# The first FFN pair by plain products over token halves, with P1 and P2 of the next two pairs between the halves

## The chip, the cores and the metric

The kernel runs on one core of a Trainium2 chip. The metric is the device time of one execution in microseconds (us), the median over several. All times below are us unless marked ns. In the profile the engines are PE (TensorE matmul), PEld (its weight loads), DVE (VectorE), ACT (ScalarE), POOL (GpSimd) and SP (SyncE), on whose queue this kernel issues its DMAs.

## The reference, cut to what matters

One layer of an encoder trunk over 1024 tokens of width 1024. Two attention branches are merged and projected, then layer norm 1 makes `x1`, then a SwiGLU FFN with 2816 hidden channels, then layer norm 2:

```
x   = layer_norm(ALPHA * x + mix, ln1_g, ln1_b)
g, u = split(x @ w_ffn_in)                 # 1024 -> 2 * 2816
ffn = (silu(g) * u) @ w_ffn_out
out = layer_norm(ALPHA * x + ffn, ln2_g, ln2_b)
```

Everything is float32. The change lies at the seam between layer norm 1 and the product `x @ w_ffn_in`.

## The kernel before

Float32 products are made of float32r operands. `split` (L102 to L104) cuts a tile into a high part, rounded by ACT (L103), and a low part, the difference, by DVE (L104). A product is then three matmuls: high by high, high by low, low by high. One such matmul has 128x128 weights and 512 columns.

The hidden channels come in 22 blocks of 128. Block f needs a left weight tile (gate, `wLf`) and a right one (up, `wRf`), each 1024 x 128. The two belong together as a pair: the 1024 input features in two halves, the tokens in two halves and the two tiles make a 2x2 block product, done with seven products P1 to P7 in place of eight (a Winograd scheme). Each product is 4 feature slices by 3 matmuls, so 12 matmuls; a pair is 84. `pair_steps` (L168) gives the seven steps in the order P1, P2, P6, P5, P7, P3, P4. P1 and P2 use only the first token half: `x1A` tiles of features 0 to 511 (A10) and 512 to 1023 (A11). P6 and P3 use sums of blocks (`x1S63`), P5 and P7 others (`x1S57`), and P4 uses `x1A22`, the second feature half of the second token half. Accumulators in PSUM are `sx` (tag "mm", two banks), `sy` and `sz` (tag "sc", two banks). The pair's results are combined in SBUF tiles `gt` and `h` (tag "yt", three slots), and `h` is stored to DRAM.

The weights need sums too. `prep_left` loads `wLf` and splits it (`wl`). `prep_right` loads `wRf`, makes `ta` and `tb` from left and right tile with four DVE subtractions (L140 to L144), and splits both (`wa`, `wb`). `prep_last` splits half of `wRf` (`wc`). The raw tiles share three slots of tag "gt", so a load waits until an earlier raw tile has had its last reader.

The seam goes so. W_out (L823 ff.) runs over eight token tiles of 128 in two passes; in the second, each token tile gets its layer norm and is stored (`x1_dr`, on SP). After token tile 3 and again after tile 7, `x1_operands` (L741) transposes four tiles to feature-major (`x1ps`, three PSUM banks of tag "tr") and makes the operands. For the first token half that is the split `x1A` tiles and a raw copy; for the second half, in four rounds `kt`, the sums `x1s13` and `x1s24` (L764 to L771), the split of `x1A22`, and the splits of both sums.

`run_pairs` (L360) then lays out the FFN's order: P1 and P2 of pair 0, P1 and P2 of pair 1, the other five steps of pair 0, the other five of pair 1, then all seven steps of pair 2 and so on. Between steps it places the weight work of later pairs. The program is written in this order, and a scheduler moves instructions within each engine's queue where their operands allow. Each engine runs its queue in order.

The lines that the change touches are `run_pairs`, `x1_operands`, `right_f`, and the calls at the seam.

Of the kernel before, what the change touches and what calls it, by code (L numbers as in the profile page):

```python
# [12 lines left out]
F32R = mybir.dt.float32r  # L13
AF = mybir.ActivationFunctionType
ALU = mybir.AluOpType
# [3 lines left out]
P = 128  # L19
# [7 lines left out]
NF = D_FF // P  # L27
# [4 lines left out]
LO, HI = slice(0, HW), slice(HW, 2 * HW)  # L32
# [14 lines left out]
def hybrid_trunk_kernel(ctx: ExitStack, tc, x, xt, w_in, b_gate, rel_bias, w_proj,  # L47
# [6 lines left out]
    nc = tc.nc  # L54
# [7 lines left out]
    def slot(tag, name, dtype=F32):  # L62
        return pool.tile([P, 1024], dtype, tag=tag, name=name, bufs=SLOTS[tag])
# [10 lines left out]
    def bank(tag, name):  # L74
        return ps.tile([P, HW], F32, tag=tag, name=name, bufs=BANKS[tag])
# [6 lines left out]
    dma = nc.sync.dma_start  # L82
# [19 lines left out]
    def split(dst_h, dst_l, src):  # L102
        nc.scalar.copy(dst_h, src)  # L103
        nc.vector.tensor_tensor(dst_l, src, dst_h.bitcast(F32), ALU.subtract)  # L104
# [22 lines left out]
    def split_w(raw, nm, tag):  # L127
        h = slot(tag, f"{nm}h", F32R)
        l = slot(tag, f"{nm}l", F32R)
        split(h, l, raw)  # L130
        return h, l
# [15 lines left out]
    def prep_last(W, nm, tag):  # L147

        c = slot(tag, f"wc{nm}", F32R)
        split(c[:, LO], c[:, HI], W["R"][:, HI])  # L150
        W["c"] = c
# [205 lines left out]

        return pair_steps(f"p{i}", Wa[i], ops_x, c, done)

    def run_pairs(steps, left, right, also=lambda i: None):  # L360

        n = len(steps)
        for i in range(n):
            if i < 2:
                for j in ((0, 1) if i == 0 else ()):
                    steps[j][0]()
                    steps[j][1]()
                rest = steps[i][2:]
            else:
                rest = steps[i]  # L370
            for j, p in enumerate(rest):
                p()
                if j == 0 and i + 1 < n:
                    right(i + 1)
                if j == 1 and i + 2 < n:
                    left(i + 2)
            also(i)
# [360 lines left out]
            done(slice(0, D))  # L738

    ops_1 = {p: [] for p in range(1, 8)}  # L740
    x1raw = []  # L741

    def x1_operands(hf, acc_t):

        for kt in range(4):
            tps = []
            for k in (kt, kt + 4):
                tp = bank("tr", f"x1ps{hf}_{k}")
                for j in range(4):
                    tr(tp[:, j * P:(j + 1) * P], acc_t[4 * hf + j][:, k * P:(k + 1) * P], ident)  # L750
                tps.append(tp)
            if hf == 0:
                raw = slot("op", f"x1raw{kt}")
                for i in range(2):
                    o = slot("xt", f"x1A1{i}_{kt}", F32R)
                    split(o[:, LO], o[:, HI], tps[i])
                    nc.scalar.copy(raw[:, (LO, HI)[i]], tps[i])
                    ops_1[1 + i].append((o[:, LO], o[:, HI]))
                x1raw.append(raw)
            else:  # L760
                raw = x1raw[kt]
                s13 = slot("kp", f"x1s13_{kt}")
                s24 = slot("kp", f"x1s24_{kt}")
                nc.scalar.copy(s13[:, LO], tps[1])  # L764
                nc.vector.tensor_tensor(s13[:, HI], raw[:, LO], tps[0], ALU.subtract)
                nc.vector.tensor_tensor(s13[:, LO], tps[0], s13[:, LO], ALU.add)
                o = slot("bw", f"x1A22_{kt}", F32R)
                split(o[:, LO], o[:, HI], tps[1])
                ops_1[4].append((o[:, LO], o[:, HI]))
                nc.vector.tensor_tensor(s24[:, LO], s13[:, LO], raw[:, LO], ALU.subtract)  # L770
                nc.vector.tensor_tensor(s24[:, HI], raw[:, HI], s24[:, LO], ALU.subtract)  # L771
                for src, pa, pb, tags in ((s24, 6, 3, ("xt",)), (s13, 5, 7, QKV)):
                    h = cycle(tags, f"x1S{pa}{pb}h_{kt}", F32R)
                    l = cycle(tags, f"x1S{pa}{pb}l_{kt}", F32R)
                    split(h, l, src)
                    ops_1[pa].append((h[:, LO], l[:, LO]))
                    ops_1[pb].append((h[:, HI], l[:, HI]))
# [8 lines left out]
    def left_f(f):  # L786
        prep_left(Wf[f], f"f{f}", w_ffn_in[f])

    def right_f(f):
        prep_right(Wf[f], f"f{f}", w_ffn_in[NF + f], ("bw", "pt")[f % 2])  # L790
        if f:
            prep_last(Wf[f], f"f{f}", "op")

    def up_steps(f):

        tl = {}

        def c(name):

            if name == "12":  # L800
                if "h" not in tl:
                    tl["h"] = slot("yt", f"h{f}")
                return tl["h"][:, LO]
            if "t" not in tl:
                tl["t"] = slot("yt", f"gt{f}")
            return tl["t"][:, LO if name == "11" else HI]

        def done(name, acc):
            if name == "11":
                nc.scalar.activation(c("11"), c("11"), AF.Silu)  # L810
            elif name == "12":
                nc.vector.tensor_tensor(c("12"), c("12"), c("11"), ALU.mult)
            elif name == "21":
                h = tl["h"]
                nc.scalar.activation(h[:, HI], acc, AF.Silu)
                nc.vector.tensor_tensor(h[:, HI], h[:, HI], c("22"), ALU.mult)
                dma(h_dr[f], h)

        return pair_steps(f"f{f}", Wf[f], ops_1, c, done)

    for half_k in range(2):
        wo = [load_w(w_out[(4 * half_k + j) * P:(4 * half_k + j + 1) * P, :], f"o{half_k}_{j}",
                     of("gt"), of("xt"), nc.vector) for j in range(4)]  # L823
        if half_k == 1:
            left_f(0)
            right_f(0)
            left_f(1)
        for tt in range(8):
            ts_ = slice(tt * P, (tt + 1) * P)
            for hf, cs in enumerate((LO, HI)):  # L830
                acc = bank("mm" if hf == 0 else "sc", f"ops{half_k}_{tt}_{hf}")
                mm3(acc, [(mh[4 * half_k + j][:, ts_], ml[4 * half_k + j][:, ts_],
                           wo[j][0][:, cs], wo[j][1][:, cs]) for j in range(4)])
                nc.vector.scalar_tensor_tensor(
                    acc_t[tt][:, cs], acc_t[tt][:, cs], ALPHA if half_k == 0 else 1.0, acc,
                    ALU.mult, ALU.add)
            if half_k == 1:
                layer_norm(acc_t[tt], g1, b1, f"1_{tt}", tt % 4 >= 2)
                dma(x1_dr[tt], acc_t[tt])
                if tt % 4 == 3:  # L840
                    x1_operands(tt // 4, acc_t)

    prep_last(Wf[0], "f0", "op")
    run_pairs([up_steps(f) for f in range(NF)], left_f, right_f)


    groups = [(0, 2), (2, 6), (6, 10), (10, 14), (14, 18), (18, 22)]
# [62 lines left out]
```

## Time and profile before

| | us |
|---|---|
| runs | 1521.20, 1521.59, 1526.46; median 1521.59 |
| the profiled execution | 1521.58, its span 1519.8 |
| PE busy | 1468.8 (97%) |
| DVE busy | 912.2 (60%) |
| ACT busy | 644.9 (42%) |
| POOL busy | 277.3 (18%) |

The profiled execution stands 0.01 us below the median of the runs, and 1.8 us of it lie outside the span. PE is the engine to look at: it is busy for 97% of the span. A busy share says little of a seam of 25 us in 1520, though. For that one follows the chain of work that ended last, the waits and the engines' rows in that window.

### The profile page before, as it was taken

What the parts mean: (1) busy time and instruction counts of PE and PEld (TensorE: products, weight loads), DVE (VectorE), ACT (ScalarE), POOL (GpSimd) and SP (SyncE); (2) the same over time, 40 slices, a digit from 0 to 9 for tenths busy, and PEclk for the clock granted to TensorE, in tenths of its full rate; (3) what the DMA queues carried; (4) which work ended last, traced back from release to release, by engine and by line L of the source; (5) the groups of instructions that cost most, each with busy time, mean ns of one, the idle gap of its engine ahead of it and who ended that gap; (6) DMA issues with size and microseconds to landing.
All of it is one profiled execution on the core that took longest, in us unless ns stands there. A gap on an engine that the chain in (4) does not pass through costs nothing.

```text
span 1519.8 us, 18815 instructions
## 1 busy us (share of the span) xinstructions
PE 1468.8 (97%) x6884; PEld 1211.4 (80%) x6884; DVE 912.2 (60%) x1496; ACT 644.9 (42%) x1108; POOL 277.3 (18%) x315
## 2 busy tenths in 40 slices
PE   8899999999999999899999899999999999999997
PEld 6688888877778888777788688888888888888886
DVE  7755553577776665665748975555555537354437
ACT  6444443677666655764403533333333334021201
POOL 0000000433355544842305000000000000000016
PEclk9999999999999999999999899999999999999999
DMA  6555546765553445757602132222222248132202
GB/s 208 152 181 167 166 133 196 211 191 167 154 155 112 125 132 159 223 195 282 231 25 82 71 119 83 83 81 84 83 83 83 83 158 291 47 125 97 70 3 109
DMA packets 60189, 205.24 MB, mean 135 GB/s; under 512 B 7728, under 2 KB 7728, under 8 KB 60096
## 3 DMA queue, kind: packets, MB, share of 16 engines
q1 hardware_dynamic: 60096, 204.03, 41.1%
q8 instruction: 54, 0.88, 0.2%
q14 instruction: 39, 0.32, 0.1%
HBM read 142.63 MB, written 61.37 MB: 134 GB/s over the span
## 4 chain that ended last, share of the span: by engine, by line
PE 48%; DVE 2%; POOL 0%; DMA 0%; issue 0%; ACT 0%; POOLq 0%; DVEq 0%; ACTq 0%
PE sxf L165 15%; PE szf L165 8%; PE fps L113 5%; PE fps L111 5%; PE fps L110 5%; PE syf L165 4%; PE ops L113 2%; PE ops L111 2%; PE ops L110 2%; DVE bn L725 0%; DVE x1S57l L104 0%; DVE acc L732 0%; DVE x1S63l L104 0%; PE x1ps L750 0%; POOL mv L728 0%; DMA ln1b<-in_ln_b_dram 0%
## 5 line engine op out<-in xcount | busy, mean ns | idle before, releaser
L728 POOL TENSOR_TENSOR mv<-mv,neghalf 128x1 f32<-128x1 f32 x16 | 23.6, 1473 | 698.0 <-DVE mv L727 698.0
L110 PE MATMUL fps<-wh_fo,wh_h 128*128 128x512 f32 x352 | 137.0, 389 | 0.0
L113 PE MATMUL fps<-wh_fo,wl_h 128*128 128x512 f32 x352 | 137.0, 389 | 0.0
L111 PE MATMUL fps<-wl_fo,wh_h 128*128 128x512 f32 x352 | 136.9, 389 | 0.0
L872 DVE TENSOR_TENSOR x<-fps,x 128x512 f32<-128x512 f32 x80 | 54.9, 688 | 95.8 <-PE fps L113 95.8
L520 POOL TENSOR_TENSOR w_b<-w_b,kp_b 128x511 f32<-128x511 f32 (+3 forms) x96 | 97.0, 1016 | 75.1 <-DVE kp_b L518 63.7
L404 PE MATMUL gps<-xl,wh_g 128*128 128x512 f32 x256 | 105.8, 413 | 0.0
L404 PE MATMUL gps<-xh,wl_g 128*128 128x512 f32 x256 | 105.8, 413 | 0.0
L404 PE MATMUL gps<-xh,wh_g 128*128 128x512 f32 x256 | 105.5, 412 | 0.0
L518 DVE TENSOR_TENSOR_SCAN kp_b<-kp_b,ident_ps 128x384 f32<-128x384 f32 (+6 forms) x88 | 78.5, 892 | 5.0
L111 PEld LDWEIGHTS fps<-wl_fo,wh_h 128*128 128x128 f32 x352 | 66.1, 188 | 13.8
L110 PEld LDWEIGHTS fps<-wh_fo,wh_h 128*128 128x128 f32 x352 | 66.1, 188 | 13.7
L113 PEld LDWEIGHTS fps<-wh_fo,wl_h 128*128 128x128 f32 x352 | 66.1, 188 | 13.6
L510 ACT ACTIVATE kp_b<-sc_b 128x512 f32<-128x512 f32 (+3 forms) x96 | 47.7, 497 | 59.8 <-PE sc_b L447 56.7
L387 ACT CAST wh_h<-wr_h 128x1024 fp32r<-128x1024 f32 x22 | 23.1, 1051 | 117.0 <-PE fps L111 91.1
L104 DVE TENSOR_TENSOR pt_b<-tp_b,pt_b 128x512 fp32r<-128x512 f32 (+1 forms) x96 | 52.0, 544 | 27.1 <-ACT pt_b L103 27.0
L514 DVE TENSOR_TENSOR_SCAN kp_b<-kp_b,ident_ps 128x128 f32<-128x128 f32 x64 | 26.7, 417 | 57.3 <-ACT kp_b L510 57.1
L485 POOL TENSOR_SCALAR w_a<-w_a,st_a 128x640 f32<-128x640 f32 (+2 forms) x64 | 42.3, 669 | 93.8 <-DVE st_a L484 77.4
L104 DVE TENSOR_TENSOR pt_a<-tp_a,pt_a 128x512 fp32r<-128x512 f32 (+1 forms) x96 | 46.4, 485 | 19.2 <-ACT pt_a L103 19.0
L165 PE MATMUL szf<-x1S63h,wcf 128*128 128x512 f32 x176 | 57.8, 389 | 0.0
L103 ACT CAST pt_b<-tp_b 128x512 fp32r<-128x512 f32 (+1 forms) x96 | 47.3, 494 | 21.8 <-PE tp_b L541 21.7
L482 ACT ACTIVATE w_a<-w_a,st_a 128x640 f32<-128x640 f32 (+2 forms) x64 | 44.5, 695 | 23.4 <-DVE st_a L477 22.5
(1445 smaller groups left out, 4110.7 us busy)
## 6 DMA issues: line engine op xcount, KB each, us to landing
wLf<-in_w_ffn_in_dram SPq DMA_DIRECT2D x22, 512.0 KB, 3.5
wRf<-in_w_ffn_in_dram SPq DMA_DIRECT2D x22, 512.0 KB, 3.5
h_dr<-h SPq DMA_DIRECT2D x22, 512.0 KB, 2.6
wr_h<-h_dr SPq DMA_DIRECT2D x22, 512.0 KB, 4.3
wr_fo<-in_w_ffn_out_dram SPq DMA_DIRECT2D x22, 512.0 KB, 4.2
v_dr<-v SPq DMA_DIRECT2D x16, 512.0 KB, 3.7
wr_g<-in_w_in_dram SPq DMA_DIRECT2D x16, 512.0 KB, 4.3
kl<-k_dr SPq DMA_DIRECT2D x32, 256.0 KB, 6.8
```

Of the source, the lines that this page charges most:

```text
L103: nc.scalar.copy(dst_h, src)
L104: nc.vector.tensor_tensor(dst_l, src, dst_h.bitcast(F32), ALU.subtract)
L110: mm(acc, lh, rh, start=(i == 0), stop=False)
L111: mm(acc, lh, rl, start=False, stop=False)
L113: mm(acc, ll, rh, start=False, stop=(i == n))
L165: mm(acc, lw[:, ks], rx, start=(first and kt == i == 0), stop=(kt == 3 and i == 2), skip_group_check=not first)
L404: mm(acc, lw[:, ks], rx[k][:, cs], start=(k == j == 0), stop=(k == KT - 1 and j == 2))
L482: nc.scalar.activation(s[:, 0:w], s[:, 0:w], AF.Exp, bias=st[:, m:m + 1], scale=-1.0, accum_out=st[:, 2:3])
L510: nc.scalar.activation(kp[:, c0:e], sc[:, 0:n], AF.Sigmoid, scale=-1.0)
L518: nc.vector.tensor_tensor_scan(kp[:, s0:e], kp[:, s0:e], ident_ps()[:, 0:e - s0], kp[:, s0 - 1:s0], ALU.mult, ALU.bypass)
L520: nc.gpsimd.tensor_tensor(be[:, m0:e], be[:, m0:e], kp[:, m0 - 1:e - 1], ALU.mult)
L872: nc.vector.tensor_tensor(acc_t[tt][:, cs], acc, acc_t[tt][:, cs], ALU.add)
```

## The change

Pair 0 is no longer made by seven products with sums. It is made by eight plain ones: for each token half, the left tile and then the right tile by all eight feature slices (`mm3`, 24 matmuls each; PSUM tiles `plainhl` and `plainhr`). So pair 0 has 96 matmuls. The first half (LO, called `plain..0f`) needs only operands that layer norm 1 gives after token tile 3. The second half (HI, `plain..512f`) needs `x1A22` and a new operand, `x1A21` (features 0 to 511 of the second token half), which `x1_operands` now splits in each of its four rounds.

The weights of pair 0 are simpler: the right tile is only split (`wrf0`), with no `ta`, `tb` and `wc`. Pairs 1 to 21 stay as they are, but `run_pairs` starts with pair 1 and gets a `then` step. The order becomes: pair 0 LO, P1 and P2 of pair 1, P1 and P2 of pair 2, pair 0 HI and its store, the other steps of pair 1, of pair 2, and pair 3. The loads of left tile 2 and right tile 1 are called ahead of that.

```diff
-    def run_pairs(steps, left, right, also=lambda i: None):
+    def run_pairs(steps, left, right, also=lambda i: None, then=lambda: None):
...
                 for j in ((0, 1) if i == 0 else ()):
                     steps[j][0]()
                     steps[j][1]()
+                if i == 0:
+                    then()
                 rest = steps[i][2:]
...
     ops_1 = {p: [] for p in range(1, 8)}
+    ops_21 = []
...
                 raw = x1raw[kt]
+                o = slot("bw", f"x1A21_{kt}", F32R)
+                split(o[:, LO], o[:, HI], tps[0])
+                ops_21.append((o[:, LO], o[:, HI]))
                 s13 = slot("kp", f"x1s13_{kt}")
...
     def right_f(f):
         prep_right(Wf[f], f"f{f}", w_ffn_in[NF + f], ("bw", "pt")[f % 2])
-        if f:
-            prep_last(Wf[f], f"f{f}", "op")
+        prep_last(Wf[f], f"f{f}", "op")
...
         if half_k == 1:
             left_f(0)
-            right_f(0)
+            R0 = slot("gt", "wRf0")
+            dma(R0, w_ffn_in[NF])
+            Wf[0]["hr"] = split_w(R0, "wrf0", "kp")
             left_f(1)
...
-    prep_last(Wf[0], "f0", "op")
-    run_pairs([up_steps(f) for f in range(NF)], left_f, right_f)
+
+    h0, gt0 = slot("yt", "h0"), slot("yt", "gt0")
+
+    def plain_half(half, x1):
+        accs = []
+        for key in ("hl", "hr"):
+            accs.append(bank("sc", f"plain{key}_{half.start}f"))
+            wh, wl = Wf[0][key]
+            mm3(accs[-1], [(wh[:, k * P:(k + 1) * P], wl[:, k * P:(k + 1) * P], *x1[k])
+                           for k in (0, 4, 1, 5, 2, 6, 3, 7)])
+        nc.scalar.activation(gt0[:, half], accs[0], AF.Silu)
+        nc.vector.tensor_tensor(h0[:, half], accs[1], gt0[:, half], ALU.mult)
+
+    def plain_rest():
+        plain_half(HI, ops_21 + ops_1[4])
+        dma(h_dr[0], h0)
+
+    plain_half(LO, ops_1[1] + ops_1[2])
+    left_f(2)
+    right_f(1)
+    run_pairs([up_steps(f) for f in range(1, NF)], lambda i: left_f(i + 1) if i > 1 else None,
+              lambda i: right_f(i + 1), then=plain_rest)
```

How the queues stand at the seam is shown at three places. In the names, the digit behind `sxf`, `syf`, `wlf` and the like is the pair, and `x1S63l_3` is the low part of that sum of round 3.

On PE, before, behind the last transposes comes P6 of pair 0:

```order
L165 MATMUL syf1_8152<-x1A11_3_7832,wlf1h_7600 128x512 x2
L165 MATMUL syf1_8152<-x1A11_3_7832,wlf1l_7601 128x512
L750 MATMUL x1ps1_7_8081<-ident_69,acc4_6948 128x128
L750 MATMUL x1ps1_7_8081<-ident_69,acc5_6949 128x128
L750 MATMUL x1ps1_7_8081<-ident_69,acc6_6950 128x128
L750 MATMUL x1ps1_7_8081<-ident_69,acc7_6951 128x128
L165 MATMUL sxf0_8107<-x1S63h_0_8012,wbf0h_7589 128x512
L165 MATMUL sxf0_8107<-x1S63l_0_8013,wbf0h_7589 128x512
L165 MATMUL sxf0_8107<-x1S63h_0_8012,wbf0l_7590 128x512
```

On PE now, the 48 matmuls of pair 0 LO, P1 of pair 1 and the first two of P1 of pair 2 have gone ahead of these rows, and this is the end of P2 of pair 1 and the start of pair 2's:

```order
L165 MATMUL syf1_8200<-x1A11_1_7784,wlf1l_7591 128x512
L165 MATMUL syf1_8200<-x1A11_2_7803,wlf1h_7590 128x512 x2
L165 MATMUL syf1_8200<-x1A11_2_7803,wlf1l_7591 128x512
L165 MATMUL syf1_8200<-x1A11_3_7822,wlf1h_7590 128x512 x2
L165 MATMUL syf1_8200<-x1A11_3_7822,wlf1l_7591 128x512
L165 MATMUL syf2_8230<-x1A11_0_7765,wlf2h_8162 128x512 x2
L165 MATMUL sxf2_8215<-x1A10_0_7761,wlf2l_8163 128x512
L165 MATMUL sxf2_8215<-x1A10_1_7780,wlf2h_8162 128x512 x2
```

What stands where P6 of pair 0 stood is P2 of pair 2, which opens a bank of tag "sc", and a matmul with the low part `wlf2l`; no block sum is read before pair 0 HI is half done.

On DVE, before, this is the end of the operand work and what follows it:

```order
L104 TENSOR_TENSOR x1S63l_2_8069<-x1s24_2_8059,x1S63h_2_8068 128x1024
L104 TENSOR_TENSOR x1A22_3_8091<-x1ps1_7_8081,x1A22_3_8091 128x512
L770 TENSOR_TENSOR x1s24_3_8087<-x1s13_3_8086,x1raw3_7827 128x512
L104 TENSOR_TENSOR x1S57l_3_8101<-x1s13_3_8086,x1S57h_3_8100 128x1024
L771 TENSOR_TENSOR x1s24_3_8087<-x1raw3_7827,x1s24_3_8087 128x512
L104 TENSOR_TENSOR wcf0_8104<-wRf0_7582,wcf0_8104 128x512
L178 TENSOR_TENSOR gt0_8120<-syf0_8122,gt0_8120 128x512
L104 TENSOR_TENSOR x1S63l_3_8097<-x1s24_3_8087,x1S63h_3_8096 128x1024
```

On DVE now, from the same subtraction on:

```order
L777 TENSOR_TENSOR x1s24_3_8089<-x1raw3_7817,x1s24_3_8089 128x512
L861 TENSOR_TENSOR h0_8106<-plainhr_0f_8133,gt0_8107 128x512
L104 TENSOR_TENSOR wlf2l_8163<-wLf2_8160,wlf2h_8162 128x1024
L104 TENSOR_TENSOR x1S63l_3_8099<-x1s24_3_8089,x1S63h_3_8098 128x1024
L140 TENSOR_TENSOR taf1_8168<-wRf1_8166,wLf1_7588 128x512
L144 TENSOR_TENSOR taf1_8168<-wRf1_8166 128x512
L141 TENSOR_TENSOR tbf1_8169<-wRf1_8166,taf1_8168 128x512
L104 TENSOR_TENSOR wcf1_8182<-wRf1_8166,wcf1_8182 128x512
L142 TENSOR_TENSOR tbf1_8169<-wLf1_7588,tbf1_8169 128x512
L178 TENSOR_TENSOR gt1_8198<-syf1_8200,gt1_8198 128x512
```

The product that reads `plainhr_0f` and so frees its bank, and the split that makes `wlf2l`, stand behind all four rounds of operand work; each round also has the new split of `x1A21`.

On ACT, before, the weight splits of pairs 1 to 3 go like this:

```order
L103 CAST waf1h_8193<-taf1_8183 128x1024
L103 CAST wcf2_8292<-wRf2_8276 128x512
L103 CAST wlf3h_8311<-wLf3_8309 128x1024
L103 CAST wbf2h_8283<-tbf2_8279 128x1024
L815 ACTIVATE h0_8179<-sxf0_8107 128x512
L103 CAST waf2h_8288<-taf2_8278 128x1024
```

On ACT now:

```order
L103 CAST waf1h_8178<-taf1_8168 128x1024
L103 CAST wcf2_8328<-wRf2_8312 128x512
L103 CAST wlf3h_8347<-wLf3_8345 128x1024
L103 CAST wbf2h_8319<-tbf2_8315 128x1024
L860 ACTIVATE gt0_8107<-plainhl_512f_8245 128x512
L103 CAST wcf3_8423<-wRf3_8407 128x512
```

The Silu that empties `plainhl_512f` stands behind the split of `tbf2`, which needs the load of the right tile of pair 2.

## Prediction

> **What bounds the kernel now.** I read the page first, then the chain of waits through the seam, then the waits, the clock and the engines' rows in that window. The page:
>
> ```profile
> span 1519.8 us, 18815 instructions
> PE 1468.8 (97%) x6884; PEld 1211.4 (80%) x6884; DVE 912.2 (60%) x1496; ACT 644.9 (42%) x1108; POOL 277.3 (18%) x315
> ```
>
> PE is busy for 97% of the span, so nearly everywhere a matmul more costs its spacing, and only PE's holes can be won. The chain of work that ended last, in order of time (start, duration, engine, tile, line), shows who owns the seam:
>
> ```profile
> 842.80 0.60 ACT x1s L764
> 844.03 0.68 DVE x1A L104
> 844.71 0.60 DVE x1s L770
> 845.31 1.14 DVE x1S57l L104
> ...
> 861.15 1.14 DVE x1S57l L104
> 862.29 0.61 DVE x1s L771
> 862.92 1.05 ACT x1S63h L103
> 864.02 0.79 PE sxf L165
> ...
> 869.70 2.72 PE sxf L165 x12
> ```
>
> From 842.8 to 862.9 the chain is DVE without a break: it makes the block sums of the second token half. Its pieces give the prices: 0.60 for 512 columns, 1.14 for 1024. After 864.0 the chain is PE alone, 12 matmuls in 2.72, so 0.2267 each. The waits of 805 to 905 (total, times, longest) name what PE missed:
>
> ```profile
> PE sxf L165 <- ACT x1S63h L103: 3.9, 2, 3.3
> PE x1ps L750 <- DVE x1s L766: 1.5, 1, 1.5
> PE sxf L165 <- ACT gt L182: 0.8, 1, 0.8
> PE sxf L165 <- DVE x1S63l L104: 0.8, 1, 0.8
> ```
>
> PE starts the FFN, and pair 3, at the first two of these rows of its timeline; the other two show what four transposes take:
>
> ```profile
> 838.07 0.70 PE L165 MATMUL sxf<-x1A,wlf0h 128*128 128x512 f32 x2
> 910.33 0.62 PE L165 MATMUL sxf<-x1A,wlf3h 128*128 128x512 f32 x2
> 848.61 0.60 PE L750 MATMUL x1ps<-ident,acc 128*128 128x128 f32 x4
> 848.97 0.48 PE L165 MATMUL syf<-x1A,wlf1h 128*128 128x512 f32 x1
> ```
>
> Between the first two lie pairs 0 to 2, 3 x 84 = 252 matmuls or 57.1, and 23 transposes at 0.09 (0.36 for four), 2.1. The 72.3 that passed hold 13.1 of loss. That is all that there is to win: 7.0 of listed waits, and most of the rest a slow clock, which the windows show (columns: PE, PEld, DVE, ACT, POOL busy with counts, granted clock, DMA share, GB/s):
>
> ```profile
> 854.00:855.00 1.00, 0.32 (x3) 0.09 (x1) 1.00 (x2) 1.00 (x2) 0.00 (x0) 0.81 0.03 8
> 858.00:860.00 2.00, 0.59 (x2) 0.19 (x1) 2.00 (x4) 1.74 (x2) 0.00 (x0) 0.99 0.00 0
> 860.00:862.00 2.00, 0.73 (x2) 0.30 (x2) 2.00 (x3) 0.00 (x0) 0.00 (x0) 0.86 0.00 0
> 862.00:864.00 2.00, 0.00 (x0) 0.00 (x0) 2.00 (x4) 1.06 (x2) 0.00 (x0) 0.50 0.00 0
> 868.00:869.00 1.00, 1.00 (x5) 0.85 (x4) 1.00 (x3) 0.22 (x2) 0.00 (x0) 0.86 0.00 0
> ```
>
> A share of 0.81 between 1.00 and 0.50 puts the fall at 854.6; likewise the clock is back at 858.0, falls at 861.4 and is back at 868.3. When the last sum lets PE go at 864.0, it runs at half speed for another 4.3, which costs 2.1. Check: 57 of the 252 matmuls are out before 864.02, the other 195 need 44.2, and 864.0 + 44.2 + 2.1 = 910.3, the row above.
>
> **The change, part by part.** The sum is made against the profiled execution, 1521.58, which is the median of the runs to 0.01.
>
> *More matmuls.* Pair 0 goes from 84 to 96: 12 x 0.2267 = +2.7, with nothing to hide behind, since PE is the chain from here to the end.
>
> *Simpler weights of pair 0.* DVE loses four subtractions and a split, ACT a split, in the second W_out pass:
>
> ```profile
> 780.00:800.00 20.00, 20.00 (x90) 16.58 (x89) 10.62 (x15) 3.16 (x3) 1.93 (x2) 1.00 0.00 1
> ```
>
> PE is busy for all 20 there and DVE for half, so this is worth 0, covered by W_out's own matmuls. In the seam `wcf0` and the addition to `gt0` go too; they stood behind DVE's last subtraction while ACT cast (862.92, above), so 0 again.
>
> *Four splits of `x1A21`.* ACT gets four casts, DVE four subtractions, at the place where DVE is the chain:
>
> ```profile
> L103 ACT CAST x1A<-x1ps x12: 587/593/623, 815.9 to 856.0; 128x512 fp32r<-128x512 f32 x12
> L104 DVE TENSOR_TENSOR x1A<-x1ps,x1A x12: 679/682/691, 816.6 to 859.9; 128x512 fp32r<-128x512 f32 x12
> ```
>
> ACT has room (0.00 in 860 to 862). DVE has none: 4 x 0.60 = +2.4. The last subtraction of the fourth round ended at 862.9 and will end at about 865.3. The weights `wrf0` also take two of the four "kp" slots that the sums rotate through, so ACT's copy for the next sum waits for the round before; the sum needs that copy three DVE operations later (1.8) and it takes ACT 0.6, so I take 0; it can only delay, and 0.5 a round, 2.0, bounds it above.
>
> *What covers DVE now.* PE's cover grows: pair 0 LO (48 matmuls), P1 and P2 of pair 1 (24) and of pair 2 (24) and pair 0 HI stand ahead of the first block sum. By count that is enough. By the queues it isn't. P2 of pair 2 opens a bank of tag "sc", of which there are two, and the last one to come free is that of `plainhr_0f`. DVE frees it with the product for `h0`, which stands behind all the operand work. So PE waits at P2 of pair 2 until 865.3 + 0.7 = 866.0. By then it has 48 + 12 + 2 + 12 = 74 matmuls out. An earlier wait, of P2 of pair 1 for the Silu of `plainhl_0f`, costs nothing more: on ACT that Silu stands ahead of the fourth round's copies, which DVE needs to end that round, so it ends earlier, and without it PE would only reach the later wait sooner.
>
> So the wait isn't removed. It has a new name and ends 2.0 later (866.0 for 864.0), with 264 - 74 = 190 matmuls left up to pair 3 where before 195 were: 866.0 + 43.1 = 909.1.
>
> *What is late next.* Four smaller waits follow, from the order on DVE and ACT:
> - `wlf2l` is DVE's next after the product, 1.2 long, ready at 867.1. PE has two matmuls (0.5) to fill that: +0.6.
> - Pair 0 HI needs the bank of P2 of pair 1, which DVE frees with its addition to `gt1`, behind `x1S63l_3` (1.14) and five weight operations (3.0): 868.2, 871.2, done 871.9. PE has 20 matmuls from 867.1, to 871.6: +0.3.
> - The right half of pair 0 HI needs the bank that the Silu of `plainhl_512f` empties, and that stands on ACT behind the split of `tbf2`. The right tile of pair 2 can be loaded once `wcf1` is done, at 870.7. These rows give the load:
>
> ```profile
> 868.29 0.33 SPq L137 DMA_DIRECT2D wRf<-in_w_ffn_in_dram  x1
> 871.95 0.62 ACT L103 CAST wcf<-wRf 128x512 fp32r<-128x512 f32 x1 [0.60 <-DMA wRf<-in_w_ffn_in_dram]
> 876.50 1.06 ACT L103 CAST wbf2h<-tbf 128x1024 fp32r<-128x1024 f32 x1 [2.24 <-DVE tbf L142]
> ```
>
>   3.7 from issue to use, so 874.4; DVE gets to it after `wbf1l` and `waf1l`, at 875.0; five operations, 878.1; the split 1.0, the Silu 0.6: 879.7. PE is there after 30 matmuls from 871.9, at 878.7: +1.0.
> - DVE's `wbf2l` now waits for a slot that `x1A21` holds until pair 0 HI has read it (some 880.5). Behind it on DVE stand four weight operations, then the `h0` product for HI, whose bank P5 of pair 1 needs. With the copy of P6 out of `sx` I put two waits of 0.25 there: +0.5.
>
> Together +2.4: pair 3 starts at 911.5 in place of 910.3, +1.2, at full clock throughout.
>
> *Clock.* PE is idle before 866.0 as it was before 864.0, so I expect the same late return, worth 2.1. But 1.3 of the small waits (+0.3 and +1.0) end at fixed times and swallow that much of it. Bounds 0 and 2.1; I take 0.6, nearer to 2.1 - 1.3 than to either end.
>
> Here the Trainium skill has a rule ("TensorE: Matmul & The Clock Gate", Part 1): the clock halves after an idle window of about 3.4 us and returns after a busy one, and the windows run free. The trace agrees: 854.6, 858.0, 861.4 and 868.3 are one, one and two such windows apart. By the rule alone PE gets 866.0 to 868.3 or to 871.7 at half speed, a loss of 1.1 or 2.8; with the 1.3 taken off the sum would be 1522.8 or 1524.3 in place of mine.
>
> *Queues.* The loads of left tile 2 and right tile 1 now pass the `x1_dr` stores on SP. Before, tile 2 came at the second row:
>
> ```profile
> 762.79 0.33 SPq L137 DMA_DIRECT2D wRf<-in_w_ffn_in_dram  x1
> 863.55 0.33 SPq L124 DMA_DIRECT2D wLf<-in_w_ffn_in_dram  x1
> ```
>
> They are 100 early, and worth 0, since the split of tile 2 stands behind DVE's operand work anyhow; without that lead tile 2's load would be one more wait, of up to 3.7. The store of `h0` stands ahead of the loads of pair 4 on SP, at some 887; pair 4's sums are due near 930, so 40 of other pairs' matmuls cover it. Worth 0. From pair 3 on PE's order is that of before.
>
> Sum: 1521.58 + 1.2 + 0.6 = 1523.4. Of the change: +2.7 for matmuls, and about 0.9 less lost at the seam than the 13.1 of before.
>
> **Rivals.**
> *A: the seam is covered.* If the banks came free in time, PE would run 264 matmuls and 23 transposes from 838.07 without a hole: 838.1 + 59.8 + 2.1 = 900.0, 10.3 ahead of before, 1511.2. For it: the count of matmuls ahead of the sums. Against: DVE's queue, in which the product stands last. It decides whether that product can run before 858, in front of the fourth round. Chance 0.03.
>
> *B: a second slow window.* The clock's changes above lie 3.4 or 6.9 apart, and in the 3.4 ahead of 854.6, cut by a wait of 1.5, the clock fell. If the wait to 866.0 and the 0.6 behind it leave the window to 868.3 too empty, half speed lasts 3.4 longer and costs 1.7 more. With the upper bound of the clock, 1521.58 + 1.2 + 2.1 + 1.7, less the 1.0 that the third wait swallows, is 1525.6. Chance 0.13. The rule of the Trainium skill cited above (same page and part) fits this: only a busy window brings the clock back.
>
> *C: slower for good.* The small waits fall one into each window up to 892 and keep the clock at half: 26 at half speed cost 13, so some 1536. Against: between 867 and 892 they sum to 1.8, and from 855.2 on PE got its clock back at 858.0 with 0.5 of holes in the window. [...] Chance 0.04.
>
> **How the numbers follow.** My forecast has 0.80, A 0.03, B 0.13, C 0.04. My forecast's own range goes from no small waits and no clock loss, 1521.6 + 1.2 - 2.4 = 1520.4, to the clock's upper bound, 1524.9; with B the upper end is near 1526. Leaving out the outer tails of both I give 1520.8 to 1526.0. About 0.5% (7.6) is what a measurement of this kernel can tell from no change: faster than 1514.0 is A alone, 0.03; slower than 1529.2 is C alone, 0.04; within, 0.93.
>
> **What would show it.** In the profile after, 74 matmuls and the transposes would bring PE to P2 of pair 2 at 857 without a wait; so its waits for ACT's Silu and for DVE's product into `h` should hold some 9 together, the second ending near 866. Then come 0.6 for `wlf2l` and about 1.0 for the Silu of the second half. `x1S63` should not be waited for. DVE should be without a hole from 842.7 to 871. Pair 3 should start at 911 to 913. I am wrong if PE passes 858 to 866 without a wait (A), or if the granted clock is 0.5 after 872 (B, C).

## The result, and the profile after

The changed kernel takes 1525.13 us in the median of 14 runs (1522.04 to 1528.53), the kernel before, measured beside it, 1522.64 (14 runs, 1520.78 to 1527.07). The ratio is 1.0012, with a 95% interval of 1.0001 to 1.0022 (the two medians alone give 1.0016): no change of a size that counts, and if any, a loss. The forecast was 1523.4, with 1520.8 to 1526.0.

The page of the profiled execution (1522.04, the fastest of the 14) answers to the one before, 12 matmuls up and PE still at 97%:

```profile
span 1520.3 us, 18836 instructions
PE 1469.8 (97%) x6896; PEld 1212.4 (80%) x6896; DVE 908.6 (60%) x1491; ACT 643.7 (42%) x1107; POOL 277.8 (18%) x315
```

The waits of 805 to 905 (total, times, longest) show that the block sums are no longer waited for. In their place stand the Silu, the product into `h` and the copy of P6:

```profile
PE syf L165 <- DVE h L861: 2.9, 1, 2.9
PE syf L165 <- ACT gt L860: 2.3, 1, 2.3
DVE wbf2l L104 <- PE plainhr_512f L113: 1.6, 1, 1.6
PE sxf L165 <- ACT h L191: 0.8, 1, 0.8
PEld sxf L165 <- DVE wlf2l L104: 0.6, 1, 0.6
```

The chain of work that ended last (start, duration, engine, tile, line) still runs on DVE, one operation behind the other, until the product into `h` and the low part of left tile 2 are made:

```profile
843.15 0.60 DVE x1A L104
...
863.09 0.60 DVE x1s L777
863.69 0.60 DVE h L861
864.29 1.13 DVE wlf2l L104
```

PE's rows (start, duration) give the seam, from the first matmul of pair 0 to the first of pair 3, and the places in it where a wait ends:

```profile
836.66 0.48 PE L110 MATMUL plainhl_0f<-x1A,wlf0h 128*128 128x512 f32 x1
864.35 1.22 PE L165 MATMUL syf<-x1A,wlf2h 128*128 128x512 f32 x2 [2.89 <-DVE h L861]
865.48 0.80 PE L165 MATMUL sxf<-x1A,wlf2l 128*128 128x512 f32 x1
871.13 0.39 PE L110 MATMUL plainhl_512f<-x1A,wlf0h 128*128 128x512 f32 x1
878.03 0.50 PE L110 MATMUL plainhr_512f<-x1A,wrf0h 128*128 128x512 f32 x1
885.08 0.50 PE L165 MATMUL szf<-x1S57h,waf1h 128*128 128x512 f32 x1
890.27 0.50 PE L165 MATMUL sxf<-x1S57h,waf1h 128*128 128x512 f32 x1 [0.76 <-ACT h L191]
910.83 0.62 PE L165 MATMUL sxf<-x1A,wlf3h 128*128 128x512 f32 x2
```

So the seam takes 910.83 - 836.66 = 74.17, where before it took 910.33 - 838.07 = 72.26: 1.9 longer. It began 1.4 earlier here, but that is no gain: in the profiles of this study it begins anywhere from 835.3 to 840.9, and within 2.7 for the changed kernel alone. Nor does anything behind the seam differ: in the three profiles of the changed kernel and the two of the one before, the device time less the place of pair 3's first matmul is 611.2 (here 1522.04 - 910.83 = 611.21). From here on I therefore compare the length of the seam, and places in it counted from its start. The wait at P2 of pair 2, "the release", ends at 27.69; before, the last block sum let PE go at 864.02 - 838.07 = 25.95.

The windows (busy time of PE, PEld, DVE, ACT, POOL with counts, granted clock, DMA share, GB/s) hold the four changes of the clock:

```profile
857.00:858.00 1.00, 1.00 (x4) 0.79 (x5) 1.00 (x3) 0.69 (x2) 0.00 (x0) 0.69 0.03 8
860.00:861.00 1.00, 1.00 (x4) 0.82 (x3) 1.00 (x2) 1.00 (x2) 0.00 (x0) 0.60 0.00 0
864.00:865.00 1.00, 0.65 (x2) 0.50 (x2) 1.00 (x2) 1.00 (x2) 0.00 (x0) 0.60 0.00 0
867.00:868.00 1.00, 1.00 (x5) 0.82 (x4) 1.00 (x3) 0.00 (x0) 0.00 (x0) 0.69 0.00 0
```

Worked out from the shares as in the prediction, the clock is halved from 857.4 to 860.8 and from 864.2 to 867.6: two stretches of 3.4, where before there were one of 3.4 and one of 6.8.

### The profile page after: what moved, and what is told of

It reads as the page before. It is cut to its first block, busy times and chain, and to the rows that moved or that the text cites. A ratio compares the mean times of both kernels' runs of the same rounds, so it can differ in the third digit from the quotient of the medians.

```text
span 1520.3 us, 18836 instructions
## 1 busy us (share of the span) xinstructions
PE 1469.8 (97%) x6896; PEld 1212.4 (80%) x6896; DVE 908.6 (60%) x1491; ACT 643.7 (42%) x1107; POOL 277.8 (18%) x315
## 4 chain that ended last, share of the span: by engine, by line
PE 46%; DVE 3%; DMA 1%; ACT 0%; issue 0%; POOL 0%; POOLq 0%; DVEq 0%; ACTq 0%
PE sxf L165 14%; PE szf L165 7%; PE fps L113 5%; PE fps L110 5%; PE fps L111 5%; PE syf L165 3%; PE ops L113 2%; PE ops L111 2%; PE ops L110 2%; DMA wRf<-in_w_ffn_in_dram 1%; DVE bn L727 0%; DVE x1S57l L104 0%; DVE x1S63l L104 0%; DVE acc L734 0%; DVE x1A L104 0%
```

## The experiments

Apart from three repeated profiles, all are edits of the changed kernel, each profiled once, so two seams that are compared are those of two single executions. A table of them ends this section. Times are us.

**Is the loss a count of matmuls, or a place in DVE's queue?** Two kernels leave out the same number of matmuls, 12, on either side of the release.

```diff
-                           for k in (0, 4, 1, 5, 2, 6, 3, 7)])
+                           for k in ((0, 4, 1, 5, 2, 6, 3, 7) if half == HI else
+                                     (0, 4, 1, 5, 2, 6))])
```

> Of the changed kernel, the first token half of pair 0 is made with 6 of its 8 products, so 12 matmuls fewer ahead of the waits (its output leaves these products out). Measured is the seam: from the first matmul of plainhl_0f to the first matmul of pair 3, 74.17 us in the changed kernel's profile. Theory (DVE's queue sets when TensorE may go on at P2 of pair 2, so matmuls ahead of that place are free): the seam stays at 74.2, within 0.4, and the two waits for the Silu (2.3) and for the product into h (2.9) together grow by about 12 x 0.2267 = 2.7, to 7.9. Rival (the seam is a count of matmuls plus a fixed loss): 74.17 - 2.72 = 71.4, and the waits stay.

The waits and PE's rows (the start of its seam is 839.40):

```profile
PE syf L165 <- DVE h L862: 2.9, 1, 2.9
PE x1ps L753 <- DVE x1s L772: 2.8, 1, 2.8
PE syf L165 <- ACT gt L861: 1.9, 1, 1.9
```

```profile
867.11 1.22 PE L165 MATMUL syf<-x1A,wlf2h 128*128 128x512 f32 x2 [2.91 <-DVE h L862]
914.87 0.62 PE L165 MATMUL sxf<-x1A,wlf3h 128*128 128x512 f32 x2
```

The release is at 867.11 - 839.40 = 27.71, the same to 0.02, and the waits have grown from 5.2 to 7.6, by 2.4 of the 2.7 taken away. The two that I had named make 4.8 and did not grow; a third, of the transposes for a bank that DVE empties, is new and 2.8 long. The seam is 75.47, not within 0.4 of the 74.17 as expected but longer. The clock was at half for 6.8 twice here. Two profiles of the changed kernel itself, shown below, also have 6.8 over the release, and seams of 75.29 and 75.91. Work taken away ahead of the release was worth nothing.

With `half == LO` in the place of `half == HI`, the 12 go behind the release:

> Of the changed kernel, the second token half of pair 0 is made with 6 of its 8 products, so 12 matmuls fewer behind the wait at P2 of pair 2 (its output leaves these products out). Theory (matmuls behind that place cost their spacing): the seam is 74.17 - 2.72 = 71.4, within 0.5, the first two waits unchanged. Rival (the later waits, for the Silu of the second half, for the product into h and for the copy of P6, end at fixed times and take up what is saved): 73 to 74, with those waits up from 1.1 to 2.5 or more.

```profile
868.19 1.22 PE L165 MATMUL syf<-x1A,wlf2h 128*128 128x512 f32 x2 [3.00 <-DVE h L862]
911.76 0.62 PE L165 MATMUL sxf<-x1A,wlf3h 128*128 128x512 f32 x2
```

The seam begins at 840.51, so the release is at 27.68 and the seam 71.25, 2.9 less than 74.17. Its second stretch of half clock was 6.8; against the profiles below that had the same, 75.29 and 75.91, it is 4.0 to 4.7 less. That is more than the spacing of 12 matmuls, 2.7, since PE's wait for the copy of P6 (0.8 in the list above, 0.7 and 1.3 in those two) is gone as well. So the rival, that later waits take the gain up, falls.

**Which bank, and which order?** `plainhr_0f` gets a bank of its own:

```diff
-            accs.append(bank("sc", f"plain{key}_{half.start}f"))
+            accs.append(bank("pv" if key == "hr" and half == LO else "sc",
+                             f"plain{key}_{half.start}f"))
```

> Of the changed kernel, the accumulator of the right tile in the first half (plainhr_0f) is put into the bank of tag pv, which nothing else uses here, in place of one of the two of tag sc. So P2 of pair 2 need not wait for the product into h. Theory (that bank is only the last piece of DVE's queue; the left tile of pair 2 comes behind the product there, and P1 of pair 2 needs its low part, ready at 865.4): the wait moves to wlf2l and to the addition into gt of pair 1, and the seam stays at 74.2, within 0.8. Rival (that bank alone holds TensorE up): most of the 2.9 and of the slow clock behind it go, and the seam is 70 to 71.

```profile
869.76 0.79 PE L165 MATMUL sxf<-x1A,wlf2l 128*128 128x512 f32 x1 [7.89 <-DVE wlf2l L104]
917.26 0.61 PE L165 MATMUL sxf<-x1A,wlf3h 128*128 128x512 f32 x2
```

As the theory has it, the wait moves: P2 of pair 2 no longer waits, but the next thing that it and P1 need, `wlf2l`, is DVE's next operation behind the product. The seam, from 840.92 on, is 76.34, over the upper end that I had given (75.0), since one idle stretch of 7.9 kept the clock at half for 10.2, from 864.8 to 875.1. A bank alone is no cure.

Now the order: the second half is written directly behind the first.

```diff
     plain_half(LO, ops_1[1] + ops_1[2])
+    plain_rest()
...
-              lambda i: right_f(i + 1), then=plain_rest)
+              lambda i: right_f(i + 1))
```

> Of the changed kernel, the second token half of pair 0 is written directly behind the first, ahead of P1 and P2 of pairs 1 and 2, instead of behind them: the part of the change that puts P1 and P2 between the halves is undone. Theory A (the place of P2 of pair 2, which needs a bank and a weight from the end of DVE's queue, is the loss): the second half needs only the bank that the Silu frees at 856.9. From there 24 + 24 matmuls, 10.9, stand ahead of P2, and DVE's product and wlf2l are over by 865.5, so one wait for the Silu of about 2.5 and a small one for the second Silu of about 1 remain: 202 matmuls from 856.9, 45.8, and 1 to 2 of waits and clock, so a seam of 67 to 68.5. Theory B (DVE's queue of block sums and operands bounds the seam whatever PE's order is; x1A of the last round comes from it at 861): the seam stays within 1 of 74.2.

```profile
838.32 0.48 PE L110 MATMUL plainhl_0f<-x1A,wlf0h 128*128 128x512 f32 x1
858.54 0.78 PE L110 MATMUL plainhl_512f<-x1A,wlf0h 128*128 128x512 f32 x1 [2.33 <-ACT gt L860]
866.57 0.50 PE L110 MATMUL plainhr_512f<-x1A,wrf0h 128*128 128x512 f32 x1 [0.69 <-ACT gt L860]
907.05 0.62 PE L165 MATMUL sxf<-x1A,wlf3h 128*128 128x512 f32 x2
```

A seam of 68.73, 5.4 less than the changed kernel's shortest and 3.5 less than before, and 0.2 over the upper end of theory A; the two waits are those of theory A. Theory B falls: DVE's product into `h` ends at 27.57 as ever, only nobody waits for it. Putting P1 and P2 of two pairs between the halves was the costly part of the change.

The last step is to give all three late accumulators a bank that is free, with the source in the changed kernel's order:

```diff
-            accs.append(bank("sc", f"plain{key}_{half.start}f"))
+            accs.append(bank("tr" if half == HI else "pv" if key == "hr" else "sc",
+                             f"plain{key}_{half.start}f"))
```

> Of the changed kernel, no accumulator of pair 0 by plain products waits for a bank: plainhr_0f stands in the one bank of tag pv, both accumulators of the second half in two of the three banks of tag tr, which the transposes have left by then, and only plainhl_0f in one of tag sc. The order of the source is that of the changed kernel. Theory (the loss is that P2 of pairs 1 and 2 and the second half queue for two banks that come free at the end of DVE's queue; with banks at hand the second half's 48 matmuls can go ahead of what needs the end of that queue): TensorE has 264 matmuls x 0.2267 = 59.9 and 23 transposes x 0.09 = 2.1 in the seam, with 0.8 of waits of the transposes for the layer norm: 62.7 to 64, no wait of over 1 us behind the transposes, no slow clock, some 10 to 11 less than the 74.17 of the changed kernel, so 9 less than before, 1512 to 1515 in all. Rival (DVE's queue of operands, 27.7 from the seam's start to its end, holds P2 of pair 2 or the first block sums anyway): a wait of 4 to 8 for wlf2l or x1S63 comes in its place, with its slow clock, and the seam is 68 to 74.

PE's rows, and the one window in which DVE's queue ends:

```profile
839.51 0.47 PE L110 MATMUL plainhl_0f<-x1A,wlf0h 128*128 128x512 f32 x1
902.82 0.62 PE L165 MATMUL sxf<-x1A,wlf3h 128*128 128x512 f32 x2
```

```profile
866.00:876.00 10.00, 10.00 (x46) 8.29 (x45) 8.44 (x12) 5.47 (x8) 0.00 (x0) 1.00 0.30 104
```

The seam is 63.31, PE has one wait in it (0.39, of the transposes for the layer norm, as before), and the clock is never halved in it. The kernel takes 1514.07 (median of 5), 0.994 of the kernel before, with an interval of 0.9925 to 0.9954: it beats both. The order that the scheduler then chooses goes with it. With banks at hand it puts 40 of the second half's 48 matmuls ahead of the first one that needs `wlf2l`; in the changed kernel all 48 stand behind it. The order alone, in the kernel above, gave 5.4 of the 10.9 that order and banks give together.

Is it the bank of `plainhr_0f` too? With that one back in "sc" and only the second half in "tr":

```diff
-            accs.append(bank("sc", f"plain{key}_{half.start}f"))
+            accs.append(bank("tr" if half == HI else "sc",
+                             f"plain{key}_{half.start}f"))
```

> Of the kernel with free banks (seam 63.31), one half alone: both accumulators of the second token half stand in banks of tag tr, but plainhr_0f stays in tag sc as in the changed kernel. Theory (the second half's banks are what matters, since with them its 48 matmuls need nothing from the end of DVE's queue and go ahead of P2 of pairs 1 and 2): most of the gain is there, a seam of 64 to 67. Rival (the gain comes from the bank of plainhr_0f together with the others): the wait for the product into h comes back with its slow clock, and the seam is 70 to 75.

```profile
839.03 0.48 PE L110 MATMUL plainhl_0f<-x1A,wlf0h 128*128 128x512 f32 x1
904.08 0.61 PE L165 MATMUL sxf<-x1A,wlf3h 128*128 128x512 f32 x2
```

65.05: 9.1 of the 10.9 come with the second half's banks.

**How much of DVE's added work is on the path?** The low part of `x1A21` is left out:

```diff
-                split(o[:, LO], o[:, HI], tps[0])
-                ops_21.append((o[:, LO], o[:, HI]))
+                nc.scalar.copy(o[:, LO], tps[0])
+                ops_21.append((o[:, LO], o[:, LO]))
```

> Of the changed kernel, DVE's four subtractions for the low part of x1A21 are left out; the second half of pair 0 reads the high part in their place (so its output lacks the low part). The number of matmuls is the same. Theory (DVE is the chain through the seam, so its four operations of 0.60 are on it in full): the product into h is over 2.4 earlier, at 25.3 from the seam's start in place of 27.7, and the seam is 71.8 to 73, since later waits take up some. Rival (DVE's rounds wait for the transposes and ACT's copies as well, so most of the 2.4 turns into waits of DVE): over at 26.5 to 27.5, and a seam of 73.5 to 74.5.

```profile
865.80 0.75 PE L165 MATMUL sxf<-x1A,wlf2l 128*128 128x512 f32 x1 [4.27 <-DVE wlf2l L104]
911.93 0.62 PE L165 MATMUL sxf<-x1A,wlf3h 128*128 128x512 f32 x2
```

The scheduler moved the product into `h` ahead of DVE's last round, so its end (19.96 from the start, 838.68) says nothing. What PE waits for last is `wlf2l`: 27.12 here, 865.48 - 836.66 = 28.82 in the changed kernel, so 1.7 of the 2.4 was on the path, between the two theories. The seam is 73.25, 0.9 less, with one stretch of 3.4 at half clock over the release in both.

**The clock.** 24 matmuls that nobody reads fill the two waits, 8 ahead of P2 of pair 1 and 16 ahead of P2 of pair 2:

```diff
+    def fill(n):
+        acc = bank("pv", f"fill{n}")
+        wh, (rh, _) = Wf[0]["hl"][0], ops_1[1][0]
+        for i in range(n):
+            mm(acc, wh[:, 0:P], rh, start=(i == 0), stop=(i == n - 1))
...
+              then_fill=[lambda: fill(8), lambda: fill(16)])
```

> Of the changed kernel, with 24 matmuls more that nobody reads, into the bank of tag pv: 8 ahead of P2 of pair 1 and 16 ahead of P2 of pair 2, to keep TensorE busy in its two long waits. Theory (a wait costs its own length and a slow clock behind it): the product into h is over at 27.7 from the seam's start as before, the granted clock stays at 1.00 or falls for one stretch fewer, the 20 matmuls behind the release take 4.5 to 5 in place of 5.65, and the smaller later waits take up some of that: seam 72.5 to 73.7. Rival (24 matmuls cost 5.4): 75 or more.

```profile
866.97 0.80 PE L165 MATMUL syf<-x1A,wlf2h 128*128 128x512 f32 x2 [1.85 <-DVE h L863]
868.10 0.79 PE L165 MATMUL sxf<-x1A,wlf2l 128*128 128x512 f32 x1 [0.34 <-DVE wlf2l L104]
913.16 0.62 PE L165 MATMUL sxf<-x1A,wlf3h 128*128 128x512 f32 x2
```

From 839.27 on, the release is at 27.70 and the seam 73.89: 24 matmuls more cost nothing, and the first stretch of half clock is gone. The second is not (867.5 to 870.9): a wait of 1.85 was left, and 20 matmuls from 868.10 took 5.98, not the 5 or less that I expected. The seam is 0.3 less than the shortest of the changed kernel and 0.2 over the theory's upper end.

The changed kernel and the one before were profiled again, as they are.

> The changed kernel itself, profiled once more, for the clock. In its first profile the clock was 0.5 from about 20.7 to 24.1 and from 27.5 to 30.9 of the seam; in the run with 12 matmuls fewer behind the wait, with the same waits up to there, the second stretch lasted twice as long. Theory (the windows in which the clock is set are not tied to the program): the waits are the same to 0.1, the release is at 27.7, and the second slow stretch is again one or two windows long, with a seam of 74.2 in the one case and 75 to 76 in the other. Rival (the clock follows the waits alone): 74.2 within 0.2 and the same stretches.

```profile
835.31 0.47 PE L110 MATMUL plainhl_0f<-x1A,wlf0h 128*128 128x512 f32 x1
862.99 1.22 PE L165 MATMUL syf<-x1A,wlf2h 128*128 128x512 f32 x2 [2.88 <-DVE h L861]
864.12 0.79 PE L165 MATMUL sxf<-x1A,wlf2l 128*128 128x512 f32 x1
871.25 0.39 PE L110 MATMUL plainhl_512f<-x1A,wlf0h 128*128 128x512 f32 x1
911.22 0.61 PE L165 MATMUL sxf<-x1A,wlf3h 128*128 128x512 f32 x2
```

```profile
862.00:863.00 1.00, 0.01 (x1) 0.01 (x1) 1.00 (x3) 0.63 (x1) 0.00 (x0) 0.79 0.00 0
866.00:869.00 3.00, 3.00 (x9) 2.32 (x8) 2.82 (x5) 0.75 (x1) 0.00 (x0) 0.50 0.26 20
869.00:870.00 1.00, 1.00 (x5) 0.82 (x4) 0.67 (x1) 1.00 (x3) 0.00 (x0) 0.80 0.58 225
```

The release is at 27.68, the waits are the same, and yet the seam is 75.91. The clock falls at 862.6 and is back only at 869.4, after 6.8. So the 20 matmuls from `wlf2l` to the second half take 7.13, where they took 5.65 in the first profile and 4.5 would be full speed.

> The changed kernel, profiled a third time. Its two profiles so far had the same waits and the release at the same place, and a second slow stretch of 3.4 in the one (seam 74.17) and of 6.8 in the other (seam 75.91). Theory (chance of the windows' phase): one of the two again, with the seam by it within 0.3. Rival (something else differs between executions): another length or another seam.

Again 6.8 of half clock, from 865.2 to 872.0, the release at 27.70, and a seam of 913.27 - 837.98 = 75.29. It misses the 75.91 by more than the 0.3 that I allowed; 0.6 of the difference is the wait of P7 for the copy of P6, 0.7 here and 1.3 there.

> The kernel before, profiled once more, for the clock. In its first profile the seam (from the first matmul of pair 0 to the first of pair 3) was 72.26, with the clock at 0.5 in two stretches, 3.4 and 6.8 long, the second from 23.4 to 30.2 of the seam, over the release at 25.95. Theory (the windows of the clock are not tied to the program): the waits and the release are the same to 0.1, and the second stretch is 3.4 or 6.8 long with other ends, the seam between 70.5 and 72.5. Rival (the clock follows the waits alone): 72.26 within 0.2 with the same stretches.

```profile
840.04 0.70 PE L165 MATMUL sxf<-x1A,wlf0h 128*128 128x512 f32 x2
912.49 0.62 PE L165 MATMUL sxf<-x1A,wlf3h 128*128 128x512 f32 x2
```

72.45, with stretches of 3.4 and 6.8 at the same places to 0.4: the kernel before looks the same twice. Two profiles can't tell whether it always does.

**The copy of P6.** It waits in the changed kernel because `h` of pair 1 takes the slot of `h0`, whose store must land first. The second profile names that landing (ACT waits 1.4 for it); the first puts the wait down to a load that was issued 0.6 behind the store. With `h0` elsewhere:

```diff
-    h0, gt0 = slot("yt", "h0"), slot("yt", "gt0")
+    h0, gt0 = slot("pt", "h0"), slot("yt", "gt0")
```

> Of the changed kernel, the tile h0 stands in a slot of tag pt in place of one of the three of tag yt, so that the copy of P6 of pair 1 need not wait until the store of h0 has landed. The scheduler now mixes pairs 1 to 3, so the place measured is the first matmul of pair 5's left tile: 112.25, 113.99 and 113.37 from the seam's start in the three profiles of the changed kernel (the first with a second slow stretch of 3.4, the others of 6.8). Theory (that copy, which waits for the landing 4.5 to 5.1 after the store's issue, costs 1.0 to 1.6 ahead of P7): no wait of P7 for it, and 1.0 to 1.6 less at the same slow stretches: 111.0 to 111.4 with 3.4, or 112.0 to 112.7 with 6.8. Rival (another wait takes its place, and it costs only the 0.25 of the prediction): 112 or 113.1 to 113.7.

```profile
893.40 0.50 PE L165 MATMUL szf<-x1S57h,waf1l 128*128 128x512 f32 x1 [0.62 <-DVE waf1l L104]
951.98 0.62 PE L165 MATMUL sxf<-x1A,wlf5h 128*128 128x512 f32 x2
```

The seam begins at 839.94, so pair 5 starts at 112.04, 0.2 earlier than the 112.25 of the profile with the same stretches. The wait is gone and another, for `waf1l`, stands there. The rival holds.

**All profiles in one view.** The last column is the time for which the clock was halved in the seam, stretch by stretch. `h0` in another slot is left out, since pairs 1 to 3 are mixed there.

| kernel | device time | start of the seam | seam | half clock |
|---|---|---|---|---|
| before | 1521.58 | 838.07 | 72.26 | 3.4, 6.8 |
| before, second profile | 1523.71 | 840.04 | 72.45 | 3.4, 6.8 |
| changed | 1522.04 | 836.66 | 74.17 | 3.4, 3.4 |
| changed, second profile | 1522.43 | 835.31 | 75.91 | 3.4, 6.8 |
| changed, third profile | 1524.48 | 837.98 | 75.29 | 3.4, 6.8 |
| 12 matmuls fewer ahead | 1526.08 | 839.40 | 75.47 | 6.8, 6.8 |
| 12 matmuls fewer behind | 1522.98 | 840.51 | 71.25 | 3.4, 6.8 |
| own bank for `plainhr_0f` | 1528.47 | 840.92 | 76.34 | 10.2 |
| second half directly behind the first | 1518.25 | 838.32 | 68.73 | 3.4 |
| three free banks | 1514.07 | 839.51 | 63.31 | none |
| free banks for the second half | 1515.32 | 839.03 | 65.05 | none |
| no low part of `x1A21` | 1523.17 | 838.68 | 73.25 | 3.4 |
| waits filled | 1524.37 | 839.27 | 73.89 | 3.4 |

Device time, less the start of the seam and the seam, is 611.2 in every row (1521.58 - 838.07 - 72.26 = 611.25 in the first, 611.20 to 611.25 in all). So what one execution differs by from another is where its seam begins and how long it is. Where the seam begins, 835.3 to 840.9, no edit here explains.

## Why the prediction was right, and where it wasn't

**The main step held.** The wait isn't removed, it gets a new name: P2 of pair 2 waits for the bank that DVE's product frees. I had it end at 866.0 - 838.07 = 27.93; it ended at 27.69, 27.68 and 27.70 in the three profiles. The two waits, for the Silu and the product, make 5.2 in the list and not the 9 that I gave. The 12 matmuls of P2 of pair 1 stand between them, from 856.86 to 861.46, and took 4.6 in place of 2.7 since the clock was halved for most of it; so 7.1 are found in these two causes. By the prediction's own count the 9 were right: 27.69, less 74 matmuls (16.8) and 23 transposes (2.1), is 8.8. That part of them was slow clock cost nothing more, since the release was set by DVE.

**The added work on DVE** (4 x 0.60 = 2.4, release 2.0 later) came out as 27.69 - 25.95 = 1.74. DVE's last subtraction of the operands ends at 863.69 - 836.66 = 27.03 from the start in the chain above, and by the prediction's chain it ended at 862.90 - 838.07 = 24.83 before, so 2.2 of the 2.4; behind it now comes the product (0.6), where before ACT's cast (1.05) came. Leaving the low parts out gave 1.7 back. (The prediction has DVE as the chain from 842.8 on; the first 0.6 of its rows are ACT's, so it is DVE's from 843.4.)

**The 12 matmuls** (+2.7, "with nothing to hide behind"). As a term of its own this was loose: ahead of the release a matmul costs nothing, which taking away 12 showed. What carried the sum was the count behind the release, 190 for 195, and that was right: 2 + 20 + 30 + 30 + 18 + 90 in the rows above.

**The small waits.** `wlf2l`: predicted 0.6, measured 1.13 - 0.45 = 0.7. The addition to `gt1` (0.3) and the Silu of the second half (1.0): 878.03 - 871.13 = 6.90 for 30 matmuls of 6.80, so 0.1 is left of the Silu, and nothing of the other can be seen; the slow clock had already used up that time. "Two waits of 0.25": 0.25 before P5, and 885.08 to 890.27 is 5.19 for 18 matmuls of 4.08, so 1.1 before P7, and 1.6 and 1.0 in the two other profiles. There I had overlooked that `h` of pair 1 takes the slot of `h0` and so waits for the landing of the store, which I had priced at 0. Its net price is 0.2 in the one profile of the last experiment, which is no more than executions of one kernel differ by.

**The clock is the step that was mis-sized.** I took 0.6 of 2.1. In the first profile the 20 matmuls behind the release lost 1.1, and the later waits took most of that back: 74.17 against 72.26 is +1.9, where I had +1.8. That these meet is in part luck: the release came 0.24 earlier than I had it, and behind it 3.4 was lost (74.17 - 27.69, less 190 matmuls) where I had 3.0 (2.4 of waits, 0.6 of clock), with the clock and P7 dearer and the Silu cheaper than I had them. In the two other profiles these matmuls lost 2.6, and the seams are 3.0 and 3.7 longer than the 72.26. This is what I had as rival B, half speed for 3.4 longer, at 1525.6 and a chance of 0.13. It came in two of three profiles of the changed kernel. Of the two kernels that keep everything up to the release and change only what is behind it, it came in one (12 matmuls fewer behind) and not in the other (`h0` in another slot). So by these few profiles B was no less likely than my forecast, and 0.13 was too low. The times don't tell the two apart. The median of 1525.13 lies nearer to B's 1525.6, but the kernel before has its median at 1522.64, 1.1 above the execution that I went from. Against that the changed kernel is up by 2.5 by the medians and by 1.8 by the ratio, and the forecast had +1.8 and B +4.0. The range and the chance of no change held because they take in both.

**Rival A**, the covered seam at 1511.2, did not come; but its condition, banks in time, was a matter of two tags. With free banks the seam is 63.31, where A had 900.0 - 838.07 = 61.9. The time, 1514.07, is 2.9 above A's: 1.4 by the seam and 1.4 by its later start. **Rival C** did not come: the clock was full from 31.0 on in the first profile and from 34.1 on in the others. Its nearest relative is the kernel with one wait of 7.9, where half speed lasted 10.2.

**The signs** were as said: `x1S63` is not waited for, DVE works without a hole to 870, the `x1_dr` stores and the early loads cost nothing that can be seen. Pair 3 at 911 to 913 is 72.9 to 74.9 from the start; the first profile's 74.17 lies in that, the other two don't. I was wrong on one sign: "the granted clock is 0.5 after 872" should show B. B's own half speed was to end at 868.3 + 3.4 = 871.7, so that sign could hardly show it; counted from the start, 872 is 33.9, and the clock was back at 34.1.

## What to carry to other kernels

In this kernel a matmul was free ahead of a release that another engine's queue sets, and cost its full spacing behind it; so count what stands on each side of the release, not the total. Where work is pulled in to cover a wait, look at which buffer it opens first: here banks that came free at the end of the very queue that was to be covered and the order that came of them cost 10.9 of the seam, the slow clock behind the waits included. One profile shows one draw of the clock: where a wait is followed by dense matmuls, profile a second time before a difference of 1 to 2 us is given a cause.

## What the runs showed of the hardware

Wherever the clock was halved in these seams, it was for whole multiples of 3.41. Over the release of the changed kernel a shift of 0.3 in where the stretch began went with one or two of them. Where the clock fell 0.11 or 0.14 ahead of the first matmul after the wait (in the first profile of the changed kernel, and with `h0` in another slot), it was back after 3.4. Where it fell 0.4 to 0.9 ahead (the second and third profile, and both kernels with 12 matmuls fewer), it stayed at half for 6.8, though from there on TensorE paused only for `wlf2l`. So a stretch with 0.4 of idle time at its start and that pause in it did not bring the clock back. The idle time at the start does not decide alone: in the kernel before, the first stretch began at 854.63, 0.53 ahead of the next matmul (855.16), and was over after 3.4. What else counts, no run here tells. And it takes less than a whole idle stretch to lose the clock: a wait of 1.85 (the filled waits) or of 2.33 was enough, one of 1.68 (without the low parts, for the Silu) or of 1.0 (only the second half's banks) was not.

The Trainium skill ("TensorE: Matmul & The Clock Gate", Part 1) gives windows of 3413 ns that run free, with a transition that varies by 500 ns either way from run to run, by where in the window the first matmul falls. The traces agree with the length (3.41, 6.83 and 10.24). They do not show that a window must be idle throughout for the clock to fall, as the rule in the prediction may be read: the waits of 1.85 and 2.33 were enough. They do not show a phase at random: in the three profiles of the changed kernel the first stretch begins at 20.72, 20.44 and 20.40 from the seam's start, while the seam itself begins anywhere within 2.7. Why the phase keeps so close to the program, no run here tells.
